# Scale and shift ahead of the experts, moved from the stored rows to the evacuation of transposed tokens

## The chip, the cores and the metric

The kernel runs on one core of a Trainium2 chip. The metric is the time on the device of one execution, in microseconds. The profile is one execution recorded by the hardware profiler. The engines are TensorE (PE, with its weight loads as PEld), VectorE (DVE), ScalarE (ACT), GpSimd (POOL) and SyncE (SP, which issues most transfers).

## What is computed

Two transformer blocks in a row on 512 tokens of 1024 features, in fp32. Each has a dense part (projections, attention or gating, an output projection with a residual) and then a mixture of experts. Where the two meet, both blocks do this:

```
x  = x + gate * (...)                       # residual
h  = rmsnorm(x, g) * (1 + scale) + shift    # gate, scale and shift: one row of 1024, from c
p  = softmax or sigmoid(h @ w_router)       # the router picks experts for each token
y  = sum over the picked experts e of  weight * (silu(h @ wg[e]) * (h @ wu[e])) @ wd[e]
x  = x + gate2 * (...y...)
```

Block 1 has 32 experts with 2 picked per token, block 2 has 64 with 8 picked and a shared expert beside them; the inner width is 256. `(1 + scale) * g` and `shift` are the same for all tokens and differ by feature. Below, they are called scale and shift.

## The kernel before, in words

**Stages.** Dense part 1 runs to about 400 us, experts 1 to about 690, dense part 2 to about 1400, experts 2 to about 2070, and a short end behind. The two *transitions* between a dense part and its experts are where the change acts. Tokens are held in four tiles of 128 rows, handled as two pairs: pair 0 is tiles 0 and 1, pair 1 is tiles 2 and 3.

**What sets the order.** Pieces of work are Python generators (`flow.start`, `yield`) which a planner interleaves by estimated costs; the result is one fixed order of instructions for each engine. Every instruction passes through one helper, so all rows of the profile name its line, L131, and are told apart by tile names, shapes and time.

**Names.** `u`, `h`, `s`, `c`, `k` are pools of working tiles (`h` also: half-width tiles of the dense part, and the transposed tokens of the router), `bank` is a PSUM bank, `hi` and `lo` the two halves into which the dense parts split an fp32 operand (`hi` on ACT, `lo`, a subtraction, on DVE), so that a product takes three matmuls. `ha_d` and `hb_d` are the DRAM copies of the tokens' rows for experts 1 and 2, `xg` a block of gathered rows, `xT` the same transposed, `iv` the indices of a block, `a` the activated inner rows, `aT` their transpose, `y` the result. `w` and `wx` are two rings of weight buffers.

**Transition.** `Post.pair` (L1820) adds the residual, computes the norm, scales the two tiles `ms` by it (one on DVE, one on ACT) and starts `Route.tile` (L1909) on each. When both tiles have been transposed there (`seen`), POOL multiplies each by the scale row and adds the shift row, in place, both rows being tiles of 128x1024 that `Post.load` (L1809) broadcast from DRAM, and stores the tile to `ha_d` or `hb_d` by a transfer of its own queue. `Route.tile` takes the tile without scale and shift: eight transposes into two banks, and each 128x128 piece leaves its bank with the scale and shift of its features as per-partition operands (`route.mod`, A and B; four pieces on ACT, four on DVE). Behind it come the router's matmuls and `pick`, a chain of small DVE and ACT instructions. In transition 2 the transposed tokens are also split into `hi` and `lo` (`keep`) for the shared expert. `choose` fixes the order of the first experts after two tiles, `finish` the rest after four.

**Experts.** For each expert `Experts.block` (L2224) builds the indices of its tokens and gathers its rows from `ha_d` or `hb_d` by an indirect transfer on POOL's queue. `Experts.xT` (L2250) transposes a block of C tokens into two banks of four features each; one ACT copy and one DVE copy take them to SBUF. `run` (L2376) then orders, per expert: gate and up matmuls 0, transposes of the previous expert's `a`, gate and up 1, down projection and result of the previous expert, `xT` of the *next* expert, gate and up 2 and 3, and the activation of the current one. Features 0 to 3 of `xT` come by ACT, and gate and up 0 and 1 read them; features 4 to 7 come by DVE. There are 32 blocks in experts 1 and 71 in experts 2. In experts 1 the loads into `wx` wait for the first gather. `ada_row` (L569) makes the rows of gate, scale and shift; each is written to DRAM, and scale and shift also stay as columns in `route.mod`.

Of the kernel before, what the change touches and what calls it, by code (L numbers as in the profile page):

```python
# [12 lines left out]
BF16 = mybir.dt.bfloat16  # L13
# [3 lines left out]
ALU = mybir.AluOpType  # L17
# [196 lines left out]
class Body:  # L214
# [316 lines left out]
    def ada_mask(self):  # L531

        nc = self.nc
        m = self.mask = self.c_const([P, 256])
        nc.gpsimd.memset(m, 1.0)
        for q in range(4):
            v = m[32 * q : 32 * q + 32].rearrange("p (i k) -> p i k", k=KD)
            nc.gpsimd.affine_select(out=v, in_=v, compare_op=ALU.is_equal, fill=0.0, base=0, pattern=[[-1, 32], [0, KD]], channel_multiplier=1)
# [30 lines left out]
    def ada_row(self, acc, b, part, dst, gain=None, plus=0.0, cols_=None):  # L569

        nc = self.nc
        cols = lambda v: v.rearrange("(p k) -> p k", k=KD)
        bc, gc, r = self.small(8), self.small(8), self.small(8) if cols_ is None else cols_
        nc.sync.dma_start(bc, cols(b[part * D : (part + 1) * D]))
        if gain is not None:
            nc.sync.dma_start(gc, cols(gain))
        yield self.at(gc if gain is not None else bc)
        nc.vector.tensor_tensor(out=r, in0=acc, in1=bc, op=ALU.add)
        if gain is not None:
            nc.vector.scalar_tensor_tensor(out=r, in0=r, scalar=plus, in1=gc, op0=ALU.add, op1=ALU.mult)  # L580
        nc.sync.dma_start(cols(dst), r)

# [89 lines left out]
    def dense1(self, x1_d, h2_d, route, x1, acc1, acc2):  # L672
# [39 lines left out]

        post = Post(self, True, mod[0:3], I["x"], x1_d, h2_d, route)
        route.mod = self.c_tile([P, 8]), self.c_tile([P, 8])

        rows = []

        def row(i):
            yield 8.0
            post.load(i, self.u)  # L720

        def ada(parts):
            for part in parts:
                acc, = yield from self.ada_sums(I["w_ada"], part, [self.cs1])
                gain = {2: (I["ln1_post"],), 4: (I["ln2_pre"], 1.0), 5: (I["ln2_post"],)}.get(part, ())
                yield from self.ada_row(acc, I["b_ada"], part, mod[part - 2], *gain, cols_={3: route.mod[1], 4: route.mod[0]}.get(part))
                if part < 5:
                    rows.append(fl.start(row(part - 2)))

# [452 lines left out]
    def dense2(self, acc_d, x2_d, route):  # L1182
# [14 lines left out]

        route.mod = self.c_tile([P, 8]), self.c_tile([P, 8])
        E = SimpleNamespace()
# [254 lines left out]
    def out2(self, mg, t_mg, x2_d, x3_d, h2_d, route, acc_d, e2):  # L1454
# [3 lines left out]
        m = self.mod2  # L1458
        post = Post(self, False, m[2:5], x2_d, x3_d, h2_d, route)
        for i in range(3):  # L1460
            post.load(i, self.r4)
        hh = [None] * NT
# [338 lines left out]
class Post:  # L1801


    def __init__(self, body, post, rows, x_d, x1_d, h2_d, route):
        self.b, self.post, self.rows, self.x_d, self.x1_d, self.h2_d = body, post, rows, x_d, x1_d, h2_d
        self.v, self.xs = [None] * 3, {}
        self.seen, self.evac = route.seen, [False] * 2

    def load(self, i, vec):  # L1809
        self.v[i] = vec()  # L1810
        self.b.bcast(self.v[i], self.rows[i])

# [7 lines left out]
    def pair(self, p, outs, then):  # L1820
        b, nc = self.b, self.b.nc
        gate, shift, scale = self.v
        xs, ms = self.xs.pop(p), [b.u() for _ in range(2)]
# [23 lines left out]
        for i in range(2):  # L1847
            if i:
                nc.scalar.activation(ms[i], xs[i], AF.Copy, scale=r[:, i : i + 1])
            else:  # L1850
                nc.vector.tensor_scalar(out=ms[i], in0=xs[i], scalar1=r[:, i : i + 1], scalar2=None, op0=ALU.mult)
            ts.append(b.flow.start(then(2 * p + i, ms[i]), MARGIN2))
        yield 1
        yield from b.wait_(lambda: self.seen >= {2 * p, 2 * p + 1})
        for i in range(2):
            nc.gpsimd.tensor_tensor(out=ms[i], in0=ms[i], in1=scale, op=ALU.mult)
            nc.gpsimd.tensor_tensor(out=ms[i], in0=ms[i], in1=shift, op=ALU.add)
            nc.gpsimd.dma_start(self.h2_d[(2 * p + i) * P : (2 * p + i + 1) * P], ms[i])
        yield from b.wait(*ts)


class Route:
# [6 lines left out]
    def __init__(self, body, E, plan, first, chosen, router, name):  # L1869
# [5 lines left out]
        self.cnt, self.orow = b.c_const([P, E]), b.c_const([P, E])  # L1875
        self.sels, self.parts, self.chosen, self.seen = [], [None] * NT, False, set()

# [31 lines left out]
    def tile(self, t, h, keep=None):  # L1909
# [4 lines left out]
        for half in range(2):  # L1914
            for j in range(4):
                nc.tensor.transpose(pts[half][:, j * P : (j + 1) * P], h[:, half * 4 + j :: KD], b.ident)
        self.seen.add(t)
        yield W
# [244 lines left out]
class Experts:  # L2163
# [86 lines left out]
    def xT(self, x):  # L2250
        b, C = self.b, x.C
        x.xT = self.xTs[x.n % len(self.xTs)]
        for half in range(2):
            pt = b.bank().rearrange("p (j q) -> p j q", j=4)
            for j in range(4):
                b.nc.tensor.transpose(pt[:, j, :C], x.xg[:C, half * 4 + j :: KD], b.ident[:C, :C])
            sl = slice(half * 4, half * 4 + 4)
            if half:
                b.nc.vector.tensor_copy(x.xT[:, sl, :C], pt[:, :, :C])
            else:  # L2260
                b.nc.scalar.activation(x.xT[:, sl, :C], pt[:, :, :C], AF.Copy)

# [337 lines left out]
```

## Time and profile before

| | us |
|---|---|
| runs | 2119.32, 2111.47, 2112.41 |
| median | 2112.41 |
| the profiled execution | 2114.14 |
| its span, first to last instruction | 2112.3 |
| PE busy in the span | 1821.3 (86%) |
| DVE, ACT, POOL busy | 999.3, 617.7, 372.8 |

The busy share is a mean over stages that differ: the experts hold long stretches in which PE and the transfers are both nearly full, the dense parts alternate between engines. What a change of one place is worth is read at that place: which wait ends last there. In a row of the timeline the bracket gives the idle time of the engine ahead of the instruction and what ended it.

### The profile page before, as it was taken

How to read it: one execution, taken by the hardware profiler on the slowest of the kernel's cores; microseconds unless marked ns; L12 is line 12 of the kernel's file. 1: busy time of each engine (PE TensorE's matmuls, PEld its weight loads, DVE VectorE, ACT ScalarE, POOL GpSimd, SP SyncE). 2: the span in 40 equal slices, each digit the busy share in tenths (PEclk: the TensorE clock that was granted, in tenths of full speed). 3: DMA queues.
4: the chain of work that ended last, by engine and by line, in shares of the span. 5: the costliest groups of instructions: out<-in, count | busy, mean ns of one | idle time of the engine just before them, and what ended most of it. 6: DMA issues, size and time to landing. Idle time of an engine off the chain costs nothing. (4 is left out here: it accounts for less than half of the span.)

```text
span 2112.3 us, 35886 instructions
## 1 busy us (share of the span) xinstructions
PE 1821.3 (86%) x13085; PEld 1162.6 (55%) x13085; DVE 999.3 (47%) x2762; ACT 617.7 (29%) x1267; POOL 372.8 (18%) x391
## 2 busy tenths in 40 slices
PE   4999977498878589889799998799999999999992
PEld 3777765354444467667677786564444444444441
DVE  5553766533222364556665646742333333333334
ACT  3523443111111242356653224321111111111111
POOL 1000002322222000000000312322222222222223
PEclk9999977599975789899999999899999999999996
DMA  8745324399999946765523655469999999999994
GB/s 336 266 161 225 134 77 166 132 354 366 378 380 380 337 177 219 244 212 149 160 68 108 213 205 210 170 230 359 365 361 358 355 346 353 359 347 364 364 329 128
DMA packets 179592, 551.81 MB, mean 261 GB/s; under 512 B 28226, under 2 KB 40642, under 8 KB 179412
## 3 DMA queue, kind: packets, MB, share of 16 engines
q1 hardware_dynamic: 158692, 491.10, 63.5%
q0 software_dynamic: 18560, 54.88, 10.5%
q10 hardware_dynamic: 2160, 3.50, 0.5%
q8 instruction: 105, 1.72, 0.3%
q14 instruction: 75, 0.61, 0.1%
HBM read 495.48 MB, written 60.53 MB: 263 GB/s over the span
## 5 line engine op out<-in xcount | busy, mean ns | idle before, releaser
L131 PE MATMUL bank<-w,xT 128*32 128x128 f32 (+5 forms) x2988 | 324.2, 365 | 10.2 <-DMA w<-in_w_gu 9.4
L131 PE MATMUL bank<-u,hi 128*128 128x512 f32 x800 | 263.1, 411 | 9.1 <-DVE u L131 5.6
L131 ACT ACTIVATE y<-bank 32x256 f32<-32x256 f32 (+5 forms) x158 | 76.5, 484 | 549.7 <-PE bank L131 525.3
L131 POOL DMA_INDIRECT acc_d<-y,iv x103 | 147.3, 1430 | 479.9 <-DVE y L131 137.2
L131 PEld LDWEIGHTS bank<-w,xT 128*32 128x32 f32 (+5 forms) x2988 | 141.2, 127 | 147.7 <-issue 101.9
L131 DVE COPY y<-bank 32x256 f32<-32x256 f32 (+5 forms) x158 | 88.3, 559 | 256.1 <-ACT y L131 210.0
L131 PE MATMUL bank<-wx,xT 128*32 128x128 f32 (+4 forms) x1812 | 187.7, 358 | 9.0 <-DMA wx<-in_w_gu 8.8
L131 PEld LDWEIGHTS bank<-u,hi 128*128 128x128 f32 x800 | 148.9, 196 | 43.8 <-DVE u L131 7.0
L131 PE MATMUL bank<-u,lo 128*128 128x512 f32 x400 | 161.4, 404 | 9.6 <-DVE lo L131 9.6
L131 PE MATMUL bank<-hi,u 128*128 128x512 f32 (+1 forms) x512 | 155.9, 389 | 2.3 <-DVE u L131 2.3
L131 DVE TENSOR_TENSOR lo<-w,hi 128x1024 fp32r<-128x1024 f32 x105 | 135.6, 1296 | 44.1 <-ACT hi L131 41.1
L131 PEld LDWEIGHTS bank<-ident,xg 48*128 48x128 f32 (+6 forms) x824 | 99.0, 200 | 75.3 <-issue 55.5
L131 PE MATMUL bank<-w,aT 128*32 128x256 f32 (+5 forms) x664 | 124.2, 522 | 13.5 <-DMA w<-in_w_dn 10.9
L131 PEld LDWEIGHTS bank<-wx,xT 128*32 128x32 f32 (+4 forms) x1812 | 85.1, 126 | 81.0 <-issue 48.7
L131 PE MATMUL bank<-wx,aT 128*32 128x256 f32 (+5 forms) x600 | 119.8, 524 | 9.1 <-DMA wx<-in_w_dn 8.7
L131 ACT ACTIVATE hi<-w 128x1024 fp32r<-128x1024 f32 x105 | 108.8, 1049 | 47.8 <-PE bank L131 24.5
L131 PE MATMUL bank<-ident,xg 48*128 48x48 f32 (+6 forms) x824 | 112.1, 280 | 10.2 <-DMA xg<-ha_d,iv 8.8
L131 PE MATMUL bank<-lo,u 128*128 128x512 f32 (+1 forms) x256 | 105.6, 413 | 16.6 <-DVE lo L131 16.1
L131 POOL TENSOR_TENSOR u<-u,t 128x1024 f32<-128x1024 f32 x16 | 41.4, 2586 | 432.3 <-DVE u L131 363.9
L131 DVE SCALAR_TENSOR_TENSOR a<-a,iv,bank 64x256 f32<-64x256 f32 (+3 forms) x80 | 38.5, 482 | 165.9 <-ACT a L131 165.9
L131 PEld LDWEIGHTS bank<-hi,u 128*128 128x128 f32 x512 | 97.8, 196 | 20.4 <-DVE u L131 3.2
L131 ACT ACTIVATE a<-bank 64x256 f32<-64x256 f32 (+4 forms) x129 | 43.3, 337 | 222.7 <-PE bank L131 212.4
(235 smaller groups left out, 2676.0 us busy)
## 6 DMA issues: line engine op xcount, KB each, us to landing
w<-in_w_gu SPq DMA_DIRECT2D x235, 512.0 KB, 13.2
wx<-in_w_gu SPq DMA_DIRECT2D x149, 512.0 KB, 12.2
w<-in_w_dn SPq DMA_DIRECT2D x101, 512.0 KB, 13.0
wa<-in_w_ada SPq DMA_DIRECT2D x96, 512.0 KB, 6.1
wx<-in_w_dn SPq DMA_DIRECT2D x91, 512.0 KB, 12.1
w<-in_w_in SPq DMA_DIRECT2D x68, 512.0 KB, 6.5
w<-in_w_out SPq DMA_DIRECT2D x21, 512.0 KB, 4.6
u<-x_d SPq DMA_DIRECT2D x12, 512.0 KB, 10.6
```

Of the source, the lines that this page charges most:

```text
L131: r = f(*a, **k)
```

## The change

The rows stored for the experts are now normed only; scale and shift are applied where a transposed block leaves its banks in `Experts.xT`, feature by feature, as the router's path does already. So the POOL arithmetic, the two broadcast rows of each transition, the wait for both tiles (`seen`) and the small stores of scale and shift to DRAM go away, and each evacuation of `xT` becomes four. `route.mod` moves to a pool that outlives the dense part, and the mask of `ada_mask` becomes bfloat16.

```diff
@@ ada_mask @@
-        m = self.mask = self.c_const([P, 256])
+        m = self.mask = self.c_const([P, 256], BF16)
@@ ada_row @@
-        nc.sync.dma_start(cols(dst), r)
+        if cols_ is None:
+            nc.sync.dma_start(cols(dst), r)
@@ dense part 1 @@
-        post = Post(self, True, mod[0:3], I["x"], x1_d, h2_d, route)
-        route.mod = self.c_tile([P, 8]), self.c_tile([P, 8])
+        post = Post(self, True, mod[0], I["x"], x1_d, h2_d, route)
+        route.mod = self.c_const([P, 8]), self.c_const([P, 8])
...
-                if part < 5:
-                    rows.append(fl.start(row(part - 2)))
+                if part == 2:
+                    rows.append(fl.start(row()))
@@ dense part 2, output @@
-        post = Post(self, False, m[2:5], x2_d, x3_d, h2_d, route)
-        for i in range(3):
-            post.load(i, self.r4)
+        post = Post(self, False, m[2], x2_d, x3_d, h2_d, route)
+        post.load(self.r4)
@@ Post.pair @@
-        gate, shift, scale = self.v
+        gate = self.v
...
+            nc.gpsimd.dma_start(self.h2_d[(2 * p + i) * P : (2 * p + i + 1) * P], ms[i])
             ts.append(b.flow.start(then(2 * p + i, ms[i]), MARGIN2))
-        yield 1
-        yield from b.wait_(lambda: self.seen >= {2 * p, 2 * p + 1})
-        for i in range(2):
-            nc.gpsimd.tensor_tensor(out=ms[i], in0=ms[i], in1=scale, op=ALU.mult)
-            nc.gpsimd.tensor_tensor(out=ms[i], in0=ms[i], in1=shift, op=ALU.add)
-            nc.gpsimd.dma_start(self.h2_d[(2 * p + i) * P : (2 * p + i + 1) * P], ms[i])
         yield from b.wait(*ts)
@@ Route.tile @@
-        self.seen.add(t)
@@ Experts.xT @@
-        b, C = self.b, x.C
+        b, C, (A, B) = self.b, x.C, self.route.mod
...
-            sl = slice(half * 4, half * 4 + 4)
-            if half:
-                b.nc.vector.tensor_copy(x.xT[:, sl, :C], pt[:, :, :C])
-            else:
-                b.nc.scalar.activation(x.xT[:, sl, :C], pt[:, :, :C], AF.Copy)
+            for k in range(4):
+                j = half * 4 + k
+                if half:
+                    b.nc.vector.tensor_scalar(out=x.xT[:, j, :C], in0=pt[:, k, :C], scalar1=A[:, j : j + 1], scalar2=B[:, j : j + 1], op0=ALU.mult, op1=ALU.add)
+                else:
+                    b.nc.scalar.activation(x.xT[:, j, :C], pt[:, k, :C], AF.Identity, scale=A[:, j : j + 1], bias=B[:, j : j + 1])
```

POOL at transition 1 (`ha_d` are the stored rows; a `-` stands in the kernel before, a `+` in the changed one):

```order
 L131 MEMSET u 128x1024
-L131 TENSOR_TENSOR u<-u 128x1024 x2
-L131 DMA ha_d<-u 128x1024
-L131 TENSOR_TENSOR u<-u 128x1024 x2
-L131 DMA ha_d<-u 128x1024
+L131 DMA ha_d<-u 128x1024 x2
 L131 MEMSET xg 128x1024 x3
-L131 TENSOR_TENSOR u<-u 128x1024 x2
-L131 DMA ha_d<-u 128x1024
-L131 TENSOR_TENSOR u<-u 128x1024 x2
-L131 DMA ha_d<-u 128x1024
```

All arithmetic between the stores is gone; the memsets of `xg` stand where they stood between the two pairs.

POOL at transition 2, from the end of pair 0 to the first gather, in the kernel before with the semaphores that each waits for (DMASW and DMAHW are transfers):

```order
L131 TENSOR_TENSOR u<-u,t_11833 128x1024 [waits Pool_49]
L131 DMA hb_d<-u 128x1024 [waits Pool_49]
L131 TENSOR_TENSOR u<-u,t_11835 128x1024 [waits DMAHW0_49,DMAHW6_49,PE_49,Activation_49]
L131 TENSOR_TENSOR u<-u,t_11833 128x1024 [waits Pool_49]
L131 DMA hb_d<-u 128x1024 [waits Pool_49]
L131 MEMSET xg 128x1024 [waits DMASW6_49]
L131 MEMSET xg 128x1024 [waits PE_49]
L131 MEMSET xg 128x1024 [waits DMAHW4_49,PE_49]
L131 DMA xg<-hb_d,iv 64x1024 [waits DMASW4_49,DMASW5_49,DMASW0_49,DMASW7_49,DVE_49,Pool_49]
```

And in the changed kernel:

```order
L131 DMA hb_d<-u 128x1024 [waits DVE_49]
L131 DMA hb_d<-u 128x1024 [waits DMASW5_49,Activation_49]
L131 DMA hb_d<-u 128x1024 [waits DVE_49]
L131 DMA hb_d<-u 128x1024 [waits Activation_49]
L131 MEMSET xg 128x1024 [waits DMAHW5_49,DMASW6_49,PE_49]
L131 MEMSET xg 128x1024 [waits DMAHW6_49,DMASW7_49,PE_49]
L131 MEMSET xg 128x1024 [waits PE_49]
L131 DMA xg<-hb_d,iv 64x1024 [waits DMASW4_49,DMASW0_49,DMASW5_49,DVE_49,Pool_49]
```

The four stores stand together, each waiting only for the engine that scaled its tile, and the first two memsets wait for stores (DMASW6, DMASW7).

DVE in an expert, before (`xT` of the next expert, then `a` of the current one):

```order
L131 COPY iv<-bank 48x1
L131 TENSOR_TENSOR iv<-bank,iv 48x1
L131 COPY y<-bank 64x512
L131 COPY xT_3582<-bank 128x4x48
L131 SCALAR_TENSOR_TENSOR a<-a,iv,bank 64x256
L131 TENSOR_TENSOR oh<-ios,R 128x192
```

And in the changed kernel:

```order
L131 COPY iv<-bank 48x1
L131 TENSOR_TENSOR iv<-bank,iv 48x1
L131 COPY y<-bank 64x512
L131 TENSOR_SCALAR xT_3568<-bank,k_320,k_321 128x48 x4
L131 SCALAR_TENSOR_TENSOR a<-a,iv,bank 64x256
L131 TENSOR_TENSOR oh<-ios,R 128x192
```

One instruction became four at the same place, ahead of the same `a`; ACT's queue has the same four in place of its one.

PE at the start of an expert, before (gate and up matmuls on `xT`, then the transposes of the previous `a`):

```order
L131 MATMUL bank<-w,xT_12856 48x256 [waits DMAHW6_49,Activation_49]
L131 MATMUL bank<-w,xT_12856 48x256 x3
L131 MATMUL bank<-ident,a 128x64 [waits DVE_49]
L131 MATMUL bank<-ident,a 128x64
L131 MATMUL bank<-w,xT_12856 48x256 [waits DMAHW7_49]
L131 MATMUL bank<-w,xT_12856 48x256 x3
```

And in the changed kernel:

```order
L131 MATMUL bank<-w,xT_13026 48x256 [waits DMAHW6_49,Activation_49]
L131 MATMUL bank<-w,xT_13026 48x256
L131 MATMUL bank<-w,xT_13026 48x256 [waits Activation_49]
L131 MATMUL bank<-w,xT_13026 48x256
L131 MATMUL bank<-ident,a 128x64 [waits DVE_49]
L131 MATMUL bank<-ident,a 128x64
```

The order is the same; the one wait for ACT's copy became a wait for each feature's piece.

## Rows read from the trace of the kernel before

**Rows 1.** Windows: busy us of each engine, granted clock, DMA share, GB/s

```profile
1320.00:1340.00 20.00, 13.71 (x53) 10.47 (x54) 14.75 (x39) 5.70 (x8) 2.80 (x2) 0.74 0.21 70
...
1400.00:2060.00 660.00, 644.69 (x5160) 309.30 (x5159) 236.78 (x798) 115.15 (x276) 171.95 (x200) 1.00 1.02 354
```

**Rows 2.** PE's waits, 1400 to 2070: us, times, longest us

```profile
PE bank L131 <- DVE a L131: 11.6, 19, 0.8
```

**Rows 3.** PE's waits, 400 to 680, first and last of four groups

```profile
PE bank L131 <- DMA w<-in_w_dn: 8.8, 13, 1.5
...
PE bank L131 <- DMA wx<-in_w_gu: 7.6, 15, 1.3
```

**Rows 4.** Timeline, transition 1, pair 0: start us, us, engine, [idle before <-releaser]

```profile
313.07 0.69 DVE L131 TENSOR_TENSOR h<-h 128x512 fp32r<-128x512 f32 x1 [0.69 <-ACT h L131]
...
331.48 2.30 DVE L131 TENSOR_TENSOR h<-h 128x512 fp32r<-128x512 f32 x1 [0.70 <-ACT h L131]
...
334.60 1.44 DVE L131 TENSOR_SCALAR s<-c,s 128x4 f32<-128x4 f32 x1
...
339.75 0.23 DVE L131 TENSOR_SCALAR s<-c,s 128x4 f32<-128x4 f32 x1
...
343.77 0.80 PE L131 MATMUL bank<-lo,h 128*128 128x512 f32 x1 [5.30 <-DVE lo L131]
```

**Rows 5.** Timeline, transition 1, pair 1, POOL and DVE

```profile
389.93 4.82 POOL L131 TENSOR_TENSOR u<-u 128x1024 f32<-128x1024 f32 x2
...
390.06 2.27 DVE L131 TENSOR_SCALAR s<-c,s 128x4 f32<-128x4 f32 x1
...
392.47 2.31 DVE L131 TENSOR_SCALAR s<-s 128x4 f32<-128x4 f32 x1
```

**Rows 6.** Timeline, transition 2, pair 0, DVE and PE

```profile
1315.17 8.21 DVE L131 TENSOR_TENSOR u<-h,u 128x512 fp32r<-128x512 f32 x4 [1.30 <-ACT u L131]
...
1326.30 0.79 PE L131 MATMUL bank<-lo,u 128*128 128x512 f32 x1 [7.86 <-DVE lo L131]
```

**Rows 7.** Timeline, transition 2, pair 1, DVE, POOL and PE

```profile
1354.70 8.57 DVE L131 TENSOR_TENSOR u<-h,u 128x512 fp32r<-128x512 f32 x4 [0.36 <-ACT u L131]
...
1360.55 0.50 PE L131 MATMUL bank<-hi,u 128*128 128x512 f32 x1 [1.72 <-DVE u L131]
...
1363.59 2.75 POOL L131 MEMSET xg<- 128x1024 f32 x3
...
1364.30 0.42 PE L131 MATMUL bank<-ident,h 128*64 128x128 f32 x1 [2.55 <-DVE h L131]
...
1364.75 1.64 DVE L131 TENSOR_SCALAR h<-h,s 128x64 f32<-128x64 f32 x1
...
1366.44 0.42 PE L131 MATMUL bank<-ident,h 128*64 128x128 f32 x1 [1.72 <-DVE h L131]
```

**Rows 8.** Evacuations: timeline (four), groups by form from 1400 to 2070 (one)

```profile
324.16 1.50 ACT L131 ACTIVATE h<-bank,c,c 128x128 f32<-128x128 f32 x4 [0.75 <-PE bank L131]
...
325.01 1.37 DVE L131 TENSOR_SCALAR h<-bank,c,c 128x128 f32<-128x128 f32 x4 [2.06 <-PE bank L131]
...
L131 ACT ACTIVATE xT<-bank 128x512 f32<-128x512 f32 x12 | 7.1, 595 | 0.7
...
L131 DVE COPY xT<-bank 128x512 f32<-128x512 f32 x12 | 8.3, 692 | 0.4
```

**Rows 9.** Timeline, one turn in experts 2, ACT and DVE

```profile
1499.47 0.33 ACT L131 ACTIVATE xT<-bank 128x192 f32<-128x192 f32 x1
...
1499.94 0.36 DVE L131 COPY xT<-bank 128x192 f32<-128x192 f32 x1
...
1500.67 0.38 ACT L131 ACTIVATE a<-bank 64x256 f32<-64x256 f32 x1 [0.87 <-PE bank L131]
...
1501.08 0.48 DVE L131 SCALAR_TENSOR_TENSOR a<-a,iv,bank 64x256 f32<-64x256 f32 x1 [0.78 <-ACT a L131]
```

More of the change, by code (lines that the diff above doesn't have):

```diff
@@ L711, in dense1, with row @@
         fl.start(bounds())
-        post = Post(self, True, mod[0:3], I["x"], x1_d, h2_d, route)
-        route.mod = self.c_tile([P, 8]), self.c_tile([P, 8])
+        post = Post(self, True, mod[0], I["x"], x1_d, h2_d, route)
+        route.mod = self.c_const([P, 8]), self.c_const([P, 8])
         rows = []
-        def row(i):
+        def row():
             yield 8.0
-            post.load(i, self.u)
+            post.load(self.u)
         def ada(parts):
@@ L1196, in ada @@
                                         cols_={3: route.mod[1], 4: route.mod[0]}.get(part))
-        route.mod = self.c_tile([P, 8]), self.c_tile([P, 8])
+        route.mod = self.c_const([P, 8]), self.c_const([P, 8])
         E = SimpleNamespace()
@@ L1801, with __init__, load @@
 class Post:
[L1804 to L1811, printed above, removed]
+    def __init__(self, body, post, gate, x_d, x1_d, h2_d, route):
+        self.b, self.post, self.gate, self.x_d, self.x1_d, self.h2_d = body, post, gate, x_d, x1_d, h2_d
+        self.v, self.xs = None, {}
+        self.evac = [False] * 2
+    def load(self, vec):
+        self.v = vec()
+        self.b.bcast(self.v, self.gate)
     def rows_of(self, p):
@@ L1875, in __init__ @@
         self.cnt, self.orow = b.c_const([P, E]), b.c_const([P, E])
-        self.sels, self.parts, self.chosen, self.seen = [], [None] * NT, False, set()
+        self.sels, self.parts, self.chosen = [], [None] * NT, False
     def setup(self):
```

## The prediction

> **What bounds the kernel now.** I read first the busy time by stretch, then what TensorE (PE) waits for in each, then the order of time around the two places where rows go from a dense part to the experts. There are three kinds of stretch. In experts 2 PE is busy for 644.69 of 660 us and the DMA share reads 1.02 [rows 1]: both are full, but PE hardly ever waits for weights there; what it waits for most is VectorE's (DVE's) `a`, 11.6 us in 19 waits [rows 2]. So experts 2 run at PE's pace, and whatever delays PE there is paid in full. In experts 1 PE waits for weights, both kinds and both matrices, four groups of waits between 7.6 and 8.8 us, some 33 us together [rows 3]: the transfers set the pace, so a small delay of PE, ACT or DVE is hidden by them, and work that ends earlier *before* the first gather moves the whole stage forward, because the transfers start with it. The dense parts are a chain PE, ACT, DVE; the change acts at their ends, while the last projection is still on PE and the routing is decided on DVE. There a DVE delay reaches PE or the first gather unless something else is later.
>
> **What the removed POOL work costs now.** Sixteen POOL tensor_tensor instructions go, eight at each transition, some 2.4 us each (two in 4.82) [rows 5]. POOL has time enough; the question is whether they disturb DVE. The rows say that they do: in each of the four pairs of tiles, DVE instructions that read SBUF last several times longer while POOL's run.
>
> *Transition 1, first pair.* The subtraction `h<-h` 128x512 takes 0.69 us at 313.07 and 2.30 at 331.48; the `s<-c,s` 128x4 takes 1.44 at 334.60 and 0.23 at 339.75 [rows 4]. The excess is 1.61 + 1.21 = 2.8 us. Both lie in the DVE queue ahead of what ends PE's wait of 5.30 us at 343.77 (DVE's `lo` stands behind the second tile's pick) [rows 4], so PE's wait shrinks by all of it. Bounds: 0, if another releaser is just as late, to 2.8.
>
> *Transition 1, second pair.* Two 128x4 instructions take 2.27 and 2.31 us, at 390.06 and 392.47, and the second ends at 394.78, the moment at which POOL's two, from 389.93 for 4.82, end at 394.75 [rows 5]. Against 0.23 [rows 4] the excess is 2.04 + 2.08 = 4.1 us. They are part of the last tiles' pick, on which the order, the indices and the first gather depend; the stage behind it runs at the transfers' pace [rows 3] and its gated weight loads start with that gather, so the 4.1 us come off its end too. Bounds: 0 (the loads do not start earlier) to 4.1.
>
> *Transition 2, first pair.* Four subtractions `u<-h,u` 128x512 take 8.21 us [rows 6] against 4 x 0.69 = 2.76 [rows 4]: excess 5.4. PE waits 7.86 us for DVE's `lo` right behind them [rows 6], long enough to give all of it back. Bounds: 0 to 5.4.
>
> *Transition 2, second pair.* The same four take 8.57 us, excess 5.8, and `h<-h,s` 128x64 takes 1.64 [rows 7]. Here PE's own waits are the cap: 1.72 + 2.55 + 1.72 = 6.0 us [rows 7]. I take 6.0, since the excess, 5.8 and what the 1.64 holds, exceeds it. Bounds: 3 (only half of the waits go, the next link being as late) to 6.0.
>
> Together 2.8 + 4.1 + 5.4 + 6.0 = 18.3 us. The wait for both tiles' transposes, ahead of the POOL work, goes too; nothing else hung on it. The stores of the rows leave right after the normalization, on the same POOL queue; at the second transition the three memsets of `xg` come behind them and now wait for two of these stores, at a place where POOL is otherwise idle and the first gather still waits for the indices.
>
> One behaviour speaks against the last two terms: POOL's memsets now come earlier and can fall beside the subtractions. In the rows a memset starts at 1363.59 for 2.75 us, and DVE's tensor_scalar at 1364.75 beside it takes 1.64 us [rows 7]; no row shows a memset beside a subtraction of two SBUF tiles. Bounds of that: 0 to 2.75 us lost; I take 0 and keep the 2.75 for the range. The Trainium skill, "SBUF — State Buffer", section "Who interferes with whom", says that a DVE instruction with two SBUF inputs contends with a GpSimd one that reads SBUF, but not with one that only writes it, while a tensor_scalar in a two-port mode contends with any. The long subtractions beside POOL's tensor_tensor and the 1.64 us beside the memset agree with that; its exemption for memsets is shown by no row here, and the sum would be the same 18.3 with it and 15.6 without.
>
> **Removed row loads.** The shift and scale rows (four 128x1024 tiles, written to DRAM as 1024 numbers each and broadcast from there) are no longer loaded. They lie in the dense parts, ahead of the places above, whose ends are set by PE, ACT and DVE, so I count 0. Upper bound: all on the path, 4 x 0.524 MB at the 354 GB/s of the fullest stretch [rows 1], 5.9 us.
>
> **What the change adds.** Each block of gathered rows was evacuated by one ACT copy and one DVE copy; now by four of each, with scale and shift. The router's tiles already leave their banks in this form: four ACT in 1.50 us, four DVE in 1.37 [rows 8]; the single copies of the same 512 columns take 0.595 and 0.692 [rows 8]. So a block costs 0.90 us more on ACT and 0.68 on DVE, nearly whatever its width, since what multiplies is the part of an instruction that does not depend on its columns. There are 71 blocks in experts 2: 64 us of ACT and 48 of DVE, beside PE. Are they covered? ACT is busy for 115.15 of 660 us and DVE for 236.78 [rows 1]. The tight place is where the copy stands right ahead of the activation of the current expert. At the tightest turn that I found, ACT's copy of 0.33 us at 1499.47 is followed by 0.87 us of idle time until `a` at 1500.67, and DVE's of 0.36 at 1499.94 by 0.78 until its `a` at 1501.08 [rows 9]. So ACT comes 0.03 us late there and DVE, with 0.68, not. Over 64 experts that is 64 x 0.03 = 1.9 us at most of what the rows show, which I take in full, as other turns have more room. Bounds: 0, to 64 us if nothing were covered. PE's first matmuls of an expert now wait for one feature block at a time, of which the first is there sooner than the single copy was; the last is used one expert's turn later, so these waits are satisfied. In experts 1 the wait for weights covers the same 0.9 us. The router's path keeps its instructions; the mask in bfloat16 changes one small operand.
>
> **The sum.** 2114.14 (the profiled execution) - 18.3 + 1.9 = 2097.7 us. The median of the runs is 1.73 us below the profiled one, so **2096.0** as a median.
>
> **The rivals.**
>
> *More, through the clock.* Behind the wait of 7.86 us the granted clock reads 0.74 between 1320 and 1340, with PE busy for 13.71 us [rows 1]; a quarter of that, 3.6 us, is what the lower of the two clock levels costs at the most. If the shorter waits keep the clock up at two or so of the four places, 7 us more go: 2089. For it: the fall comes right behind a long wait. Against: waits of 2 to 3 us remain at the same places.
>
> *Part of it lost in experts 2.* If the idle time ahead of `a` is less than it looks (each of four instructions pays its own release), PE waits perhaps 0.15 us longer per expert: 64 x 0.15 = 9.6 us, 2105.6. For it: 19 waits for `a` exist already [rows 2]. Against: they are short, and ACT stands idle ahead of most `a`.
>
> *The stalls are not POOL's, or the next link is as late.* Then about nothing changes: 2112 to 2114. Against: the two instructions that end with POOL's, to 0.03 us [rows 5].
>
> *Slower.* The eight evacuations take the place of the stall: ACT's 0.90 us per block comes onto PE's path in every expert, through `a`, its transpose and the down projection. At 0.5 us per expert it costs 64 x 0.5 = 32 us, of which 1.9 is in the sum: 2096.0 + 30.1 = 2126.1. It eats the whole gain at 18.3 / 64 = 0.29 us per expert, and decides from 0.45 on, (18.3 + 10.6) / 64. For it: experts 2 have no other slack on PE [rows 1], and the activations of `a` wait in the same queues. Against: 0.87 and 0.78 us of idle time at the tightest turn [rows 9]. The Trainium skill, "VectorE: DVE Perf Modes", section "The TRN2 errata — SBUF-src ops pay a fixed extra latency per instruction", states a fixed cost per instruction and advises tiles of 512 elements or more, which speaks against splitting one evacuation into four. By its table three more from PSUM would cost an estimated 375 ns on DVE and 430 on ACT per block; the rows' 0.68 and 0.90 us, which hold the operands of scale and shift too, are worse, and I use them.
>
> **How the numbers follow.** A measurement of this kernel can tell about 0.5% from no change, 10.6 us: faster is below 2101.9, slower above 2123.0. The forecast, with terms that may each fall short, runs from 2091 to 2102 and gets 0.62; the clock 0.13; the part lost in experts 2 0.12; nothing 0.05; slower 0.08. Faster is 0.62 + 0.13 = 0.75, the same 0.12 + 0.05 = 0.17, slower 0.08. The range reaches from 2087, past the clock's case, to 2106, past the partial loss; outside lie "nothing" and "slower", 0.13, and tails.
>
> **What would show it.** In the changed kernel's rows the subtractions 128x512 should all take about 0.69 us and the 128x4 0.16 to 0.23; the PE waits of 5.30 and 7.86 should be near 2.5; the first gathers should come 7 and some 18 us earlier from the start; experts 1 and 2 should last as long as before, within 2 us. PE waits for `a` above some 20 us in experts 2 would show the loss; a PE wait for another engine as long as before at a transition would show that the stall was not the last link. I am wrong if subtractions stay long beside memsets or transfers from the POOL queue, or if experts 2 grow by more than 8 us.

## The result

The changed kernel takes **2094.78 us** (median of 6 runs, 2085.76 to 2102.56) against 2112.36 us for the kernel before in the same comparison (6 runs). The ratio is 0.991, 95% interval 0.9888 to 0.9931: some 17.6 us less. The forecast was 2096.0, with a range of 2087 to 2106. The profiled execution took 2096.3 us, with a span of 2094.3 us. One run of the kernel before in r4 below took 2558.95 us, at a mean granted clock of 0.645 where all others read 0.92 to 0.94, and no ratio holds it.

### The profile page after: what moved, and what is told of

It reads as the page before. It is cut to its first block, busy times and chain, and to the rows that moved or that the text cites. A ratio compares the mean times of both kernels' runs of the same rounds, so it can differ in the third digit from the quotient of the medians.

```text
span 2094.3 us, 36484 instructions
## 1 busy us (share of the span) xinstructions
PE 1821.3 (87%) x13085; PEld 1162.2 (55%) x13085; DVE 1048.0 (50%) x3071; ACT 709.2 (34%) x1576; POOL 333.6 (16%) x375
## 3 DMA queue, kind: packets, MB, share of 16 engines
q8 instruction: 105, 1.72, 0.3%
## 5 line engine op out<-in xcount | busy, mean ns | idle before, releaser
L131 PE MATMUL bank<-u,hi 128*128 128x512 f32 x800 | 262.3, 410 | 11.4 <-DVE u L131 5.6
L131 PE MATMUL bank<-wx,xT 128*32 128x128 f32 (+4 forms) x1812 | 197.3, 377 | 4.4 <-DMA wx<-in_w_gu 3.0
L131 PE MATMUL bank<-u,lo 128*128 128x512 f32 x400 | 161.3, 403 | 11.6 <-DVE lo L131 11.6
L131 PE MATMUL bank<-hi,u 128*128 128x512 f32 (+1 forms) x512 | 151.6, 380 | 0.5 <-DVE u L131 0.5
L131 ACT ACTIVATE xT<-bank,k,k 128x32 f32<-128x32 f32 (+6 forms) x412 | 132.5, 405 | 29.8 <-PE bank L131 27.0
L131 PEld LDWEIGHTS bank<-wx,xT 128*32 128x32 f32 (+4 forms) x1812 | 89.6, 132 | 80.2 <-issue 55.0
L131 DVE TENSOR_SCALAR xT<-bank,k,k 128x32 f32<-128x32 f32 (+6 forms) x412 | 113.3, 339 | 27.3 <-PE bank L131 15.1
L131 PEld LDWEIGHTS bank<-hi,u 128*128 128x128 f32 x512 | 94.9, 190 | 17.2 <-DVE u L131 0.9
L131 POOL DMA_INDIRECT xg<-hb_d,iv x71 | 70.8, 998 | 203.6 <-PE bank L131 83.5
```

Source lines behind the costliest of these rows:

```text
L131: r = f(*a, **k)
```

## Profile after, beside the rows of before

The page's first lines: span, and busy time of each engine.

```profile
span 2094.3 us, 36484 instructions
## 1 busy us (share of the span) xinstructions
PE 1821.3 (87%) x13085; PEld 1162.2 (55%) x13085; DVE 1048.0 (50%) x3071; ACT 709.2 (34%) x1576; POOL 333.6 (16%) x375
```

PE is busy for the same 1821.3 us as before; the 18 us are idle time of PE that went. POOL lost 39 us, and ACT gained 92 and DVE 49 through the split evacuations. With the split alone and POOL's arithmetic still there (r2 below) DVE is busy for 1068.5 us, so 20.5 us of DVE's busy time went with the arithmetic.

Transition 1, pair 0, timeline: DVE's subtractions, two of its `s<-c,s`, and the end of PE's wait. These answer to [rows 4].

```profile
325.46 0.43 DVE L131 TENSOR_TENSOR hc<-h,hc 128x256 fp32r<-128x256 f32 x1 [0.48 <-ACT hc L131]
...
327.18 0.69 DVE L131 TENSOR_TENSOR h<-h 128x512 fp32r<-128x512 f32 x1 [0.70 <-ACT h L131]
...
328.69 0.23 DVE L131 TENSOR_SCALAR s<-c,s 128x4 f32<-128x4 f32 x1
...
332.63 0.23 DVE L131 TENSOR_SCALAR s<-c,s 128x4 f32<-128x4 f32 x1
...
336.65 0.79 PE L131 MATMUL bank<-lo,h 128*128 128x512 f32 x1 [3.91 <-DVE lo L131]
```

The 2.30 and 1.44 us of [rows 4] are 0.69 and 0.23 here, the values that the same instructions had before where POOL stood still; PE's wait of 5.30 us is 3.91. The first line is that of a subtraction which [rows 4] leaves out; in the kernel before it lay beside POOL's arithmetic too, ahead of the same wait:

```profile
329.02 1.16 DVE L131 TENSOR_TENSOR hc<-h,hc 128x256 fp32r<-128x256 f32 x1 [0.48 <-ACT hc L131]
```

Transition 1, pair 1, the pick of the pair's first tile on DVE, as in [rows 5]:

```profile
381.45 0.23 DVE L131 TENSOR_SCALAR s<-c,s 128x4 f32<-128x4 f32 x1
...
381.82 0.16 DVE L131 TENSOR_SCALAR s<-s 128x4 f32<-128x4 f32 x1
```

0.23 and 0.16 us stand where 2.27 and 2.31 stood.

Transition 2, the subtractions on DVE and PE's waits of pair 1, as in [rows 6, 7]:

```profile
1306.69 2.49 DVE L131 TENSOR_TENSOR u<-h,u 128x512 fp32r<-128x512 f32 x4
...
1339.97 1.28 DVE L131 TENSOR_TENSOR u<-h,u 128x512 fp32r<-128x512 f32 x2
...
1343.79 1.29 DVE L131 TENSOR_TENSOR u<-h,u 128x512 fp32r<-128x512 f32 x2 [2.54 <-DMA x_d<-u]
...
1344.54 0.50 PE L131 MATMUL bank<-hi,u 128*128 128x512 f32 x1 [0.48 <-DVE u L131]
...
1346.12 0.30 PE L131 MATMUL bank<-ident,h 128*64 128x128 f32 x1 [0.39 <-DVE h L131]
...
1346.57 0.64 DVE L131 TENSOR_SCALAR h<-h,s 128x64 f32<-128x64 f32 x1
...
1347.27 0.30 PE L131 MATMUL bank<-ident,h 128*64 128x128 f32 x1 [0.84 <-DVE h L131]
...
1348.58 0.25 DVE L131 TENSOR_SCALAR h<-h,s 128x64 f32<-128x64 f32 x1
```

Four subtractions take 2.49 us, and two pairs of them 1.28 and 1.29, in place of 8.21 and 8.57. Behind the first four PE has no wait of note any more (7.86 us before). PE's three waits of 1.72, 2.55 and 1.72 us have become 0.48, 0.39 and 0.84. One row is disturbed still: `h<-h,s` 128x64 takes 0.64 at 1346.57 and 0.25 two us later; POOL's memsets of `xg` lie there. And a next link shows: the last two subtractions now stand idle for 2.54 us until a transfer, `x_d<-u`, is done.

Experts 2: the stretch that answers to the second of [rows 1], PE's longest waits (to [rows 2]), and one turn on ACT and DVE (to [rows 9]).

```profile
1390.00:2050.00 660.00, 644.38 (x5168) 307.20 (x5168) 280.05 (x992) 175.21 (x482) 167.77 (x136) 1.00 1.02 353
```

```profile
PE bank L131 <- DVE a L131: 11.8, 19, 1.1
...
PE bank L131 <- DMA xg<-hb_d,iv: 2.3, 2, 2.0
```

```profile
1478.17 1.24 ACT L131 ACTIVATE xT<-bank,k,k 128x48 f32<-128x48 f32 x4
...
1478.64 1.03 DVE L131 TENSOR_SCALAR xT<-bank,k,k 128x48 f32<-128x48 f32 x4
...
1479.36 0.38 ACT L131 ACTIVATE a<-bank 64x256 f32<-64x256 f32 x1
...
1479.78 0.48 DVE L131 SCALAR_TENSOR_TENSOR a<-a,iv,bank 64x256 f32<-64x256 f32 x1
```

PE is busy for 644.38 of 660 us (644.69 before), and waits for `a` 19 times and 11.8 us (11.6). In the tight turn ACT's four pieces end at the moment `a` starts, and DVE's 0.11 us ahead of it: the idle time of 0.87 us is used up, that of 0.78 nearly. From the start of ACT's evacuation to `a` it is 1.19 us, and 1.20 before, so nothing is delayed.

**Where the time went, by stretches.** Four markers stand in every profile: the first transposes of pair 0 at each transition (PE, `ident,u`), and the first and last gather of each experts stage (POOL, `xg`). At the transitions they read, with the first transposes of pair 1 as well, before and after:

```profile
323.00 3.68 PE L131 MATMUL bank<-ident,u 128*128 128x128 f32 x16 [10.85 <-DVE u L131]
...
382.21 3.65 PE L131 MATMUL bank<-ident,u 128*128 128x128 f32 x16 [14.15 <-DVE u L131]
...
409.83 1.04 POOL L131 DMA_INDIRECT xg<-ha_d,iv  x1 [13.98 <-DVE iv L131]
...
1310.02 2.06 PE L131 MATMUL bank<-ident,u 128*128 128x128 f32 x16 [0.87 <-DVE u L131]
...
1350.54 2.02 PE L131 MATMUL bank<-ident,u 128*128 128x128 f32 x16 [2.62 <-DVE u L131]
...
1381.07 1.04 POOL L131 DMA_INDIRECT xg<-hb_d,iv  x1 [14.74 <-DVE iv L131]
```

```profile
319.43 3.68 PE L131 MATMUL bank<-ident,u 128*128 128x128 f32 x16 [10.85 <-DVE u L131]
...
373.60 3.65 PE L131 MATMUL bank<-ident,u 128*128 128x128 f32 x16 [12.88 <-DVE u L131]
...
398.08 1.04 POOL L131 DMA_INDIRECT xg<-ha_d,iv  x1 [23.07 <-DVE iv L131]
...
1301.69 3.68 PE L131 MATMUL bank<-ident,u 128*128 128x128 f32 x16 [2.38 <-DVE u L131]
...
1335.01 3.63 PE L131 MATMUL bank<-ident,u 128*128 128x128 f32 x16 [2.56 <-DVE u L131]
...
1360.38 1.04 POOL L131 DMA_INDIRECT xg<-hb_d,iv  x1 [13.22 <-DVE iv L131]
```

So transition 2 took 1381.07 - 1310.02 = 71.05 us and takes 1360.38 - 1301.69 = 58.69. The same for all stretches and profiles, in us (labels are those of the experiments below):

| profile | to trans. 1 | trans. 1 | experts 1 | dense 2 | trans. 2 | experts 2 | end |
|---|---|---|---|---|---|---|---|
| before | 323.0 | 86.8 | 263.4 | 636.8 | 71.1 | 661.9 | 69.4 |
| before, again (r4) | 320.0 | 85.0 | 264.7 | 640.4 | 70.7 | 662.5 | 68.9 |
| after | 319.4 | 78.7 | 261.6 | 642.0 | 58.7 | 663.0 | 70.9 |
| after, again (r0) | 322.8 | 76.4 | 262.6 | 640.8 | 58.5 | 662.4 | 69.4 |
| mask only (r5) | 319.6 | 85.0 | 264.1 | 640.5 | 71.2 | 662.4 | 69.2 |
| split alone (r2) | 319.6 | 85.0 | 261.5 | 639.5 | 71.0 | 662.2 | 72.3 |
| split alone (r10) | 321.0 | 85.0 | 261.4 | 633.2 | 70.8 | 661.0 | 72.1 |
| single copies (r1) | 319.3 | 78.0 | 262.5 | 641.5 | 57.4 | 660.7 | 100.2 |
| rows back (r6) | 321.4 | 78.9 | 261.9 | 638.4 | 58.6 | 661.7 | 69.2 |
| idle arithmetic (r3) | 320.8 | 79.7 | 262.4 | 645.1 | 63.8 | 663.0 | 72.7 |
| idle arithmetic 2 (r7) | 321.2 | 82.1 | 261.3 | 639.6 | 68.3 | 663.1 | 69.9 |
| idle memsets (r9) | 319.5 | 78.2 | 262.3 | 638.4 | 58.0 | 662.5 | 71.1 |
| evacuated twice (r8) | 321.1 | 78.7 | 263.1 | 634.8 | 57.6 | 687.5 | 69.8 |

In the row of the single copies, experts 2 are taken to the 71st gather, as in the others; this kernel has a 72nd, 37.6 us later. But for the two runs with idle arithmetic, which lie between, transition 2 falls in two groups, 70.7 to 71.2 and 57.4 to 58.7, and transition 1 too, 85.0 to 86.8 and 76.4 to 78.9. Dense part 2 scatters by 12 us over kernels that differ little there. A gain must therefore be read at its place: the sum over one pair of profiles holds several us of scatter.

## The experiments

**The changed kernel again (r0).** No edit.

> The changed kernel once more, unedited, as the mark for the other runs on the same chip and as a second profile of it. Theory (stalls beside POOL's arithmetic are gone): about 2095 us again, 17 below the kernel before. The profile before shows a granted clock of 0.83 between 260 and 280 us, the profile after 1.00 in the same stretch, and the 3.2 us that this is worth lie ahead of anything that the change touches: if that is chance, this second profile may show either.

Measured: 2092.36 us (6 runs), ratio 0.9891 (0.987 to 0.9911). The fall of the clock at 260 to 280 us is in this profile too:

```profile
260.00:280.00 20.00, 18.76 (x124) 15.32 (x122) 10.20 (x42) 13.53 (x38) 0.00 (x0) 0.83 0.55 185
```

In the first profile of after, the same stretch reads 1.00. So the 3 us there are chance, and no part of the gain.

**Single copies (r1): the addition undone.**

```diff
-            for k in range(4):
-                j = half * 4 + k
...
+            sl = slice(half * 4, half * 4 + 4)
+            if half:
+                b.nc.vector.tensor_copy(x.xT[:, sl, :C], pt[:, :, :C])
+            else:
+                b.nc.scalar.activation(x.xT[:, sl, :C], pt[:, :, :C], AF.Copy)
```

> The changed kernel with the single ACT and DVE copy per block of xT put back; scale and shift of the experts' rows are left out, so the experts compute on normed rows only. It undoes the addition and keeps the removal. Theory (0.90 and 0.68 us per block are covered but for 1.9 us in all): 1 to 3 us below the changed kernel on the same chip, about 2093. Rival (the eight evacuations are partly on PE's path): 8 us or more below it, 2087 or less. In experts 2 PE's waits for a should fall by at most 2 us by the theory.

Measured: 2120.46 us (9 runs), and neither theory had that. The reason lies in the edit: without scale and shift block 1 gives other values, so the router of block 2 picks other experts, and a block of tokens more than planned is worked through at the very end. The gathers of experts 2 in this profile and in that of r0:

```profile
L131 POOL DMA_INDIRECT xg<-hb_d,iv x72 | 72.0, 1000 | 199.6 <-PE bank L131 122.7 <-DVE iv L131 41.7 <-issue 35.2
```

```profile
L131 POOL DMA_INDIRECT xg<-hb_d,iv x71 | 71.1, 1001 | 199.6 <-PE bank L131 86.8 <-DVE iv L131 78.6 <-issue 34.3
```

72 stand against 71, and the end stretch is 100.2 us against 69 to 73. The total says nothing, then. Up to the 71st gather the blocks have the same widths as before, so the stretches can be compared: experts 2 take 660.7 us, 1.7 to 2.3 less than in the two profiles of the changed kernel, and PE waits 11.1 us for `a`, 0.7 less.

**The split evacuation alone (r2 and r10), twice the same kernel.**

```diff
-            sl = slice(half * 4, half * 4 + 4)
...
+            for k in range(4):
+                j = half * 4 + k
...
```

The new lines are those of the change; A and B are constants here, 1 and 0, and the mask is in bfloat16.

> The kernel before with the evacuation of xT in four ACT and four DVE pieces, with constants 1 and 0 as scale and shift (the mask in bfloat16 to make room); POOL's arithmetic stays, and the result is the same. It does the addition alone. Theory: 1 to 3 us above the kernel before, 2113.5 to 2115.5. Rival (evacuations on the path): 10 us or more above it, over 2122. A third possibility, that the pieces help because PE's first matmul gets its features sooner: below 2112.

> The kernel before with the split evacuation alone, a second time. The first came out 0.2% below the kernel before (0.35% to 0.07%), where 1 to 3 us above was expected. Its profile has experts 1 at 261.5 us from the first to the last gather where three profiles with single copies have 263.4 to 264.7. Theory (PE's finer waits gain some 2 us in experts 1, and experts 2 cost 0 to 1): 1 to 3 us below the kernel before, and again 261 to 262.5 in experts 1. Rival (chance): no difference, and experts 1 at 263.5 or more.

Measured: 2108.23 us, ratio 0.9979 (0.9965 to 0.9993), and the second time 2112.44 us, ratio 1.0 (0.9985 to 1.0016), 12 runs each. The first lay where only the expectation's third possibility had it, the second shows no change. Two comparisons of one kernel thus differ by 0.2%, so that their intervals only just overlap; that is the resolution here. The stretches agree better: experts 1 take 261.4 and 261.5 us in both, against 263.4 to 264.7 in the three profiles of before and of the mask alone. That the finer waits are the cause of these 2 us is not shown, for in the changed kernel single copies (r1) give 262.5, and the split 261.6 and 262.6.

The end stretch takes some 3 us more in both, and the traces show where: of the last three indirect stores of `y` on POOL's queue, the first leaves 25.1 and 24.8 us behind the last gather (22.6 and 22.5 in the two profiles of before), and the last one 35.3 and 35.0 (33.1 and 33.0). The first profile of the changed kernel has the late stores too (24.9 and 35.3), the second (21.7 and 33.2) and r6 (21.7 and 33.2) have not, so the split alone does not decide it; what held the store was not followed. In experts 2 the addition costs -1.5 to +0.3 us against the kernel before. Within the resolution the addition is neutral.

**The mask alone (r5) and the kernel before again (r4).**

```diff
-        m = self.mask = self.c_const([P, 256])
+        m = self.mask = self.c_const([P, 256], BF16)
```

> The kernel before with nothing but the mask in bfloat16. The kernel with the split evacuation alone, which has this mask too, came out 4 us below the kernel before where 1 to 3 above was expected. Theory (the mask is no cause: its 16 multiplications take 417 ns with either type): within 1.5 us of the kernel before, 2111 to 2114. Rival (the mask, or the place that it frees, gives the 4 us): 2107 to 2109.

> The kernel before, unedited, for a second profile of it. In the first one dense part 2 took 636.8 us from the last gather of experts 1 to the first transposes of transition 2, and three profiles of kernels with the change 640.8 to 642.0. Theory (chance, by stretches in which the granted clock fell): this profile lies somewhere between 636 and 643 in that stretch, and its fall at 260 to 280 us may be gone. Rival (the change makes dense part 2 some 4 us longer): 637 again. The transitions should repeat: 104 us from 305 to the first gather, 71.0 from the transposes to the first gather of experts 2.

Measured: 2112.25 us for the mask (ratio 1.0009, 0.9994 to 1.0024) and 2114.01 for the kernel before against itself (1.0018, 0.9997 to 1.0038). No effect of the mask is seen. (The runs r4 to r7 were made on another chip than the rest, each with the kernel before beside it.) The second profile of before has 640.4 us in dense part 2, so the change does not lengthen that part.

**The broadcast rows back (r6).**

```diff
-        post = Post(self, True, mod[0], I["x"], x1_d, h2_d, route)
+        post = Post(self, True, mod[0:3], I["x"], x1_d, h2_d, route)
...
-        post.load(self.r4)
+        for i in range(3):
+            post.load(i, self.r4)
```

> The changed kernel with the four broadcast rows of scale and shift and their small stores put back; nobody reads them. Theory (they cost nothing of their own): within 1.5 us of the changed kernel, about 2092 to 2095. Rival, after the first runs: at transition 1 the first square of the second pair starts 1.3 us earlier in all kernels without these rows than in those with them, since the rotating tiles u come free sooner; then this gives 1.3 us back there and as much again at most elsewhere, 2095 to 2097. All four loads on the path would be 6 us, 2099.

Measured: 2093.75 us (6 runs), ratio to before 0.9927 (0.9913 to 0.994), where the changed kernel had 0.991 and 0.9891. The transitions are the changed kernel's (78.9 and 58.6 us), and no stretch is longer by more than 0.2 us. So the rows cost nothing that shows, as counted; a cost of 4 us in all would not stand out between two comparisons.

**Idle arithmetic on POOL (r3, r7).** The arithmetic is done again at its old places, and nobody waits for it; r3, whose edit stands here, reads one tile twice; in r7 the second operand is the gate's row, `in1=self.v`.

```diff
+            yield from b.wait_(lambda: self.seen >= {2 * p, 2 * p + 1})
+            for i in range(2):
+                for _ in range(2):
+                    nc.gpsimd.tensor_tensor(out=self.junk, in0=ms[i], in1=ms[i], op=ALU.mult)
```

> The changed kernel with POOL's sixteen multiplications of 128x1024 put back at their old places, reading the stored tiles and writing to a tile that nobody reads; the stores go ahead of them. The work is there again, and nothing waits for its result. Theory (DVE is stalled while POOL's arithmetic runs): the gain goes back, 2110 to 2114, and the subtractions 128x512 beside them take 2 us again in place of 0.69. Rival (the gain is that the rows are stored earlier, or that a wait on POOL's result went): it stays at about 2095.

> As the run with idle arithmetic, but each of POOL's multiplications reads two different tiles (the stored tile and the gate's row), as in the kernel before; with one tile read twice they took 1.97 to 2.12 us each in place of 2.4, and half of the gain came back. Theory (DVE loses the time for which POOL's arithmetic lies beside its subtractions): now about 2.4 us each and three quarters or more of the 12.4 us at transition 2 come back, 66.5 to 70 us from the transposes to the first gather of experts 2 where the first such run had 63.8 and the changed kernel 58.6; in all 2102 to 2108. Rival (half of the gain is not the stall but the stores' earlier start): 63.8 again, and 2100.

Measured: r3 2100.72 us (10 runs; 0.9946, 0.9928 to 0.9965), r7 2106.01 us (12 runs; 0.9979, 0.9964 to 0.9995). r3 gave back less than the theory said; r7 shows why. Transition 2 of r3, POOL's arithmetic of pair 0, and the subtractions:

```profile
1309.33 8.49 POOL L131 TENSOR_TENSOR t<-u 128x1024 f32<-128x1024 f32 x4
...
1312.10 6.87 DVE L131 TENSOR_TENSOR u<-h,u 128x512 fp32r<-128x512 f32 x4 [0.36 <-ACT u L131]
...
1349.61 3.84 DVE L131 TENSOR_TENSOR u<-h,u 128x512 fp32r<-128x512 f32 x2 [0.33 <-ACT u L131]
...
1354.65 1.70 DVE L131 TENSOR_TENSOR u<-h,u 128x512 fp32r<-128x512 f32 x2 [1.21 <-DMA x_d<-u]
```

And of r7, POOL, the subtractions, and PE:

```profile
1305.61 10.38 POOL L131 TENSOR_TENSOR t<-u,t 128x1024 f32<-128x1024 f32 x4
...
1308.39 8.75 DVE L131 TENSOR_TENSOR u<-h,u 128x512 fp32r<-128x512 f32 x4 [0.35 <-ACT u L131]
...
1318.17 0.42 PE L131 MATMUL bank<-ident,h 128*64 128x128 f32 x1 [5.59 <-DVE h L131]
```

In r7 POOL's four take 10.38 us and the subtractions 8.75, as long as before the change, and PE waits 5.59 us behind them. In r3 POOL was done sooner, with 8.5 us a pair, and some of the subtractions had become free: 6.87, and 3.84 + 1.70 us for four. Transition 2 takes 68.3 us in r7, inside the 66.5 to 70 of the theory, so 9.7 of the 12.4 us that it gained are the stall itself, with no result awaited and no store delayed. Transition 1 takes 82.1 us in r7, between the two groups. What the other 2.7 us of transition 2 hang on is not shown; one difference that is seen is PE's last wait in the second pair, behind `h<-h,s` and a memset, 1.72 us before and 0.86 in r7.

**Idle memsets on POOL (r9).**

```diff
+            for i in range(2):
+                for _ in range(5):
+                    nc.gpsimd.memset(self.junk, 0.0)
```

> The changed kernel with ten POOL memsets of 128x1024 at each of the four places where the idle arithmetic stood, about 0.92 us each, so as long as the arithmetic was; they write a tile that nobody reads, and read nothing. It asks which DVE instructions a POOL instruction that only writes stalls. Theory (two SBUF operands on DVE collide with what POOL reads): the subtractions u<-h,u of transition 2 stay at 2.5 us for four as in the changed kernel, transition 2 stays at 58 to 60 us, and the whole at 2092 to 2097; the small tensor_scalar instructions of transition 1's second pair, which have one SBUF operand, may be stalled by one memset, up to 0.9 us each. Rival (any POOL work on SBUF stalls DVE): subtractions of 8 us, transition 2 at 66 us or more, 2104 to 2110. The Trainium skill, page SBUF — State Buffer, section Who interferes with whom, says the former.

Measured: 2094.69 us (4 runs), ratio 0.9929 (0.9901 to 0.9956). The changed kernel's time, with 10 us of POOL work beside each pair. Transition 2, POOL and the subtractions, and two small instructions of transition 1's second pair, which lie beside memsets as well:

```profile
375.24 10.05 POOL L131 MEMSET u<- 128x1024 f32 x10
...
381.42 0.87 DVE L131 TENSOR_SCALAR s<-s 128x4 f32<-128x4 f32 x1
...
385.45 0.16 DVE L131 TENSOR_SCALAR s<-s 128x4 f32<-128x4 f32 x1
...
1299.79 10.06 POOL L131 MEMSET t<- 128x1024 f32 x10
...
1302.59 2.50 DVE L131 TENSOR_TENSOR u<-h,u 128x512 fp32r<-128x512 f32 x4 [0.36 <-ACT u L131]
```

The subtractions, of two SBUF tiles, are not touched: 2.50 us for four. The tensor_scalar `s<-s` 128x4 is: 0.87 at 381.42, beside memsets, and 0.16 at 385.45, behind them. So it is not that POOL works, but what the two engines do: POOL's arithmetic stalls DVE's subtractions, POOL's memset does not, and a memset can stall a small tensor_scalar. The Trainium skill, "SBUF — State Buffer", section "Who interferes with whom", says the same: a DVE instruction with two SBUF inputs contends with a GpSimd one that reads SBUF and not with one that only writes it, and a tensor_scalar in a two-port mode contends with GpSimd. The prediction had left the memset beside a subtraction open, with 2.75 us for it.

**Every evacuation twice (r8).**

```diff
-            for k in range(4):
+            for k in (0, 1, 2, 3, 0, 1, 2, 3):
```

> The changed kernel with every evacuation of xT made twice (eight ACT and eight DVE pieces a block, the same values written again): another 1.50 us of ACT and 1.37 of DVE at 128 columns a piece, on top of the first excess of 0.90 and 0.68. In three pairs of profiles the first excess cost 0 to 2 us in experts 2. Theory (it is covered by the idle time ahead of a, 0.87 us at the tightest turns and about 2 us at most others): the tight turns now pay up to 1.5 us each, a third of 64 turns, and the others little: 15 to 35 us above the changed kernel, 2110 to 2130, with PE's waits for a in experts 2 well above 20 us in place of 12. Rival (ACT and DVE have far more room than the idle time ahead of a says): within 5 us of the changed kernel. Other rival (nothing is covered): 71 x 1.5 = 106 us.

Measured: 2116.71 us (10 runs), ratio 1.0026 (1.0013 to 1.004), 22 us above the changed kernel and about the time of the kernel before. PE's waits in experts 2:

```profile
PE bank L131 <- DVE a L131: 16.7, 27, 1.3
...
PE bank L131 <- DVE oh L131: 7.3, 10, 1.3
...
PE bank L131 <- ACT xT L131: 6.5, 14, 1.3
```

Waits for `a` go from 11.8 to 16.7 us, less than the 20 expected, and two others come: `oh`, from which the next block's indices are made, and `xT` itself. The three grow by 18.3 us together. Experts 2 take 687.5 us, 24.5 more than in the profile after. So the slower rival's mechanism is real, and its point lies between one and two such excesses: the first excess, ACT busy for 60 us more in the 71 blocks (175.21 against 115.15), is covered, and the next, another 78 us or 1.1 a block (250.45 from 1375 to 2042 against 172.01 from 1375 to 2023 in the profile after), costs 24.5 / 64 = 0.38 us per expert.

## Why the prediction was right, point by point

- **Transition 1, pair 0**: 2.8 us forecast. From the first transposes to PE's `lo` the time went from 343.77 - 323.00 = 20.8 us to 336.65 - 319.43 = 17.2: 3.6 us. The mechanism is the one named, and the 0.8 us beyond the term are a third stalled instruction that the prediction did not count, the subtraction `hc<-h,hc` 128x256, 1.16 us at 329.02 and 0.43 now: 1.61 + 1.21 + 0.73 = 3.55. The prediction took its 2.8 us off PE's wait of 5.30; that wait fell by 1.4 only, to 3.91 where some 2.5 were said, and the other 2.2 us came ahead of it, where PE ends its earlier matmuls sooner.
- **Between the pairs** nothing was forecast and 1.1 to 1.5 us were gained (382.21 - 343.77 = 38.4 us, and 38.1 in the second profile of before, against 373.60 - 336.65 = 37.0): the second pair's norm starts sooner behind the projection. Its first DVE instruction starts 2.02 us behind PE's last matmul before, and 0.76 after. ACT's first two squares show why it can: before, the first starts at 367.63, 0.44 us ahead of the end of the projection's last matmul, and now at 358.66, 2.06 us ahead of it, so that it no longer waits for what the second one needs. It is there with the rows back (r6) and with idle arithmetic (r3, r7). That is as far as the cause was followed. From the first to the second transposes it took 59.2 and 58.9 us in the two profiles of before and takes 54.2 and 54.4.
- **Transition 1, pair 1**: 4.1 forecast. The two rows went to 0.23 and 0.16 as said, but from the second transposes to the first gather the first profile of after gained only 27.6 - 24.5 = 3.1 us on the first profile of before, and 1.6 on the second one. The granted clock differs there: it reads 0.50 at 380 to 390 in the first profiles of before and of after, the lower of the two levels (1.2 GHz of 2.4) throughout, and 0.67 in the second profiles, r4 and r0, which differ by 26.1 - 22.0 = 4.1 us. Between profiles of like clock the term holds within 1 us.
- **Transition 2**: 11.4 forecast, 12.4 measured. The first pair gave 7.2 (1350.54 - 1310.02 less 1335.01 - 1301.69) where 5.4 stood, the second 5.2 (the rest of the stretch) where 6.0 stood. The 1.8 us more in the first lie within the 3.6 that the clock's rival put on this place at the most: the 20 us behind PE's wait read 0.74 before [rows 1], and the same work, some 10 us earlier, reads 1.00 now. That the clock gave them is not shown, and elsewhere it took something: the sixteen transposes of the second pair take 3.63 us (3.53 in r0) where they took 2.02. In the second pair the term itself was too large: PE's three waits gave 4.3 of their 6.0 us. The last of them, 1.72, stood behind `h<-h,s`, which lay beside a memset that stays [rows 7], so it was not the arithmetic's to give; it fell to 0.84.

```profile
1310.00:1330.00 20.00, 19.67 (x93) 15.32 (x93) 16.76 (x41) 8.27 (x12) 0.00 (x0) 1.00 0.38 140
```

- **Experts 1**: their start came earlier and they kept it, as forecast, and ended 1 to 3 us sooner still (261.6 and 262.6 us against 263.4 and 264.7), where nothing was forecast. The finer waits may be the cause; single copies in r1, with 262.5, do not bear it out.
- **Experts 2**: 1.9 us forecast as a cost, and 0 to 2 measured (663.0 and 662.4 against 661.9 and 662.5; single copies in r1 660.7). The reading of the tight turn was exact: idle time 0.87, excess 0.90, and nothing left over on ACT in the profile after.
- **Row loads at 0** and **memsets at 0**: both held, the first within some 4 us (r6), the second for the subtractions (r9).
- **The clock's rival** (7 us more) did not come as a whole: a part of it may be in transition 2, and low levels remain at both transitions. **Partial loss** and **slower** did not come, for the reason given; r8 shows that the second is a real edge, at most 1.1 us of ACT a block further on.

Over the means of two profiles of each kernel, transition 1 gained 8.4 us, transition 2 12.3 and experts 1 2.0, and experts 2 lost 0.5; dense part 2 lost 2.8 and the end 1.0, by scatter as far as is known. The two comparisons gave 17.6 and 20.6. So the places are right and each term nearly so, but that the total came within 1.3 us of the forecast is in part luck: gains that were not forecast, at transition 1 and in experts 1, stand against losses elsewhere. The first gathers came 11.8 and 20.7 us earlier in the first two profiles, where 7 and some 18 were forecast; 3.6 us of both lie ahead of transition 1 and are chance.

## What to carry to other kernels

An engine that is idle for four fifths of the time can still cost, by the instructions that it stalls on its neighbour: compare the duration of one and the same instruction inside and outside the other's spans before calling its work hidden. What is moved onto an engine with room should be measured against the idle time right ahead of the instruction that PE waits for, not against the engine's mean share; here 0.9 us of ACT a block fitted and 2.0 did not. And a gain of under 1% is read at its place, between two markers, with two profiles of each kernel.

## What the runs showed of the hardware that was not expected

- POOL's tensor_tensor 128x1024 on one tile read twice takes 8.49 us for four (r3), on two different tiles 10.38 (r7), both beside the same subtractions: 2.1 and 2.6 us each.
- A low granted clock came and went at the same place in executions of one kernel (0.83 and 1.00 at 260 to 280 us, in both kernels), worth some 3 us.
- Evacuations from PSUM are not stalled by POOL's arithmetic: DVE's four `h<-bank,c,c` 128x128 take 1.37 us at 325.01 [rows 8], where POOL's first two run from 325.12 for 4.79, and 1.37 at 321.45 in the profile after, with POOL idle.
- Two comparisons of one kernel, 12 runs each, gave 0.9979 (0.9965 to 0.9993) and 1.0 (0.9985 to 1.0016) against the same kernel before: 0.2% between two comparisons is no difference here.
